# A transformer step on one core: u and v in program order, the matvec's finishing step moved, and ACT's weight conversions queued behind attention's copies

## Chip, core and metric

The kernel runs on one core of a Trainium2 chip. The metric is the device time of one execution in microseconds; before the change three runs took 1706.94, 1707.95 and 1711.22 us, median 1707.95. A separate execution was profiled; it took 1710.82 us.

## What is computed

One layer of a hybrid backbone for 128 context tokens and 256 latent tokens, 384 in all, model width 2048, in float32:

```python
mod = silu(cond) @ ada_w + ada_b            # 6 vectors of 2048 for each of two conditions
h   = rmsnorm(x, norm_w[0]) * (1 + scale_a) + shift_a
q, k, v, o, g, u = split(h @ w_in)          # 8 heads x 128, 32 gates, 1024 pooled channels
hm  = bidirectional_mlstm(q, k, v, g) ; hm = rmsnorm(hm) * sigmoid(o)
hp  = centred_pooling(u) @ pool_w * pool_scale
x   = x + gate_a * rmsnorm(concat(hm, hp) @ w_out, norm_w[1])
h   = rmsnorm(x, norm_w[2]) * (1 + scale_f) + shift_f
y   = square(relu(h @ w1)) @ w2             # hidden width 8192
x   = x + gate_f * rmsnorm(y, norm_w[3])
```

The outputs are x for all tokens and the final states of the mLSTM of the context tokens.

## The kernel before

Every large product is done in three fp32r products: the weights and the activations are each split into a rounded part `hi` and a rest `lo`, and `hi*hi`, `hi*lo` and `lo*hi` are added up in PSUM (`mm3`, L140). For the weights `load_w` (L120) does this for each tile of 128 x 1024: a DMA issued by SP into one of three `raw` buffers, a copy on ACT that rounds (L132), a subtraction on DVE (L133); there are four buffers (`N_W`) of `hi` and four of `lo`. So the conversion of a tile can begin when PE is through with the tile four before it.

**u and v (L391 to L423).** The work on w_in's columns u and v runs in 8 steps of 256 rows (two k of 128). Each step has five chunks of columns: u0, u512 (512 columns), v0, v3 (3 heads of 128) and v6 (2 heads and the 32 gates). A chunk is 18 matmuls: two k, three token tiles, three products. Its sums are added to SBUF by DVE (by ACT in step 0). Before a step can begin, its 256 rows of h must be there: `make_h` (L355) multiplies x by `mod` and adds the shift, on DVE (`hm`, L361; `hl`, L367) and ACT (`hh`, L366).

Those values of `mod` come from a matvec on PE with `ada_w`, a generator (`ada_mat`, L209) that is advanced by `next(ada0)`. Nine calls make one step's worth: eight load one piece of 512 KB each (four buffers) and multiply it on PE (8 small matmuls, L226); with the eighth comes the copy of the sums to `ada_sb` on ACT (L232); the ninth, here called the finishing step, does four more matmuls on `ada_sb` (L235) and adds up `mod` on DVE (L243, L248). `ADA_STEPS = (4, 0, 5, 0, 0)` says how many calls come behind each chunk: four behind u0, five behind v0. `make_h` of the next step is written behind the matmuls of v3 (`ci == 3`).

**Who orders the instructions.** The opening of the kernel, up to `order.close()` (L388), is inside a `manual_schedule` of PE, DVE and ACT: these engines do what is written there in the order in which it is written. Outside, a planner orders each engine's instructions ahead of time, from costs and due times, in the main by their place in the program. Every engine then executes its own list in order: an instruction that waits holds all that stands behind it in the list of its engine. `tc.issue_after(ins)` asks that what is written under it comes behind `ins` in the list of that engine.

The transposes of x (`transpose_x`, L327: three on PE per k, one copy on ACT or DVE) for the last seven k stand behind `order.close()`.

**q, k, o and what is fed between (L164, L696 to L742).** `gemm_T` goes through a product in tiles of 24 matmuls; after each tile it calls `feeds`, generators that add other work. While q and k of heads pair g are computed, the feeds do the gates and the pooling (g = 0), or the attention of the pair before (`attention`, L556): `decays` (matmul `mb`, L573; exponentials on ACT, L575), scores, state updates (`update`, L607; the sums of the context tokens are copied from PSUM by ACT to `C`, L615), outputs, and in the ninth call a transpose to `hT` with a copy by ACT to `hnT` (L686). The gates' generator (L463) transposes `aS`, `bS` and `gS` in its third call (`ps_col`, L527), which need exponentials that ACT does in its second.

Of the kernel before, what the change touches and what calls it, by code (L numbers as in the profile page):

```python
# [9 lines left out]
AF = mybir.ActivationFunctionType  # L10
# [5 lines left out]
KT = D // P  # L16
NTOK = 384
# [10 lines left out]
N_W = 4  # L28
N_ADA = 4
N_E = 1  # L30
ADA_STEPS = (4, 0, 5, 0, 0)
X_ORDER = "tatatatabtatatatat"
N_X = 4
RATE_GF = 0.4
RATE_GS = 0.25
S_FIRST, S_LAST, N_LAST = 1, 6, 2
RATES = (1.5, 1.3, 1.3)
RATE_MAT = 0.35

# [2 lines left out]
def hymba_kernel(  # L42
# [6 lines left out]
    nc = tc.nc  # L49
# [13 lines left out]
    def bank(name):  # L63
        return psum.tile([P, 512], F32, tag="ps", name=name)
# [50 lines left out]
    mw = prmT[:, 64:72]  # L115
# [4 lines left out]
    def load_w(pieces, name, n=1024, after=(), later=None):  # L120

        raw = wp.tile([P, 1024], F32, tag="raw", name=f"raw_{name}", bufs=3)
        a = pieces[0][1].shape[1]
        rv = raw[:, 0:n].rearrange("p (a b) -> p a b", a=a)
        for off, src in pieces:
            load_w.ins = nc.sync.dma_start(rv[:, :, off:off + src.shape[2]], src).ins
        hi = wp.tile([P, 1024], F32R, tag="hi", name=f"hi_{name}", bufs=N_W)
        lo = wp.tile([P, 1024], F32R, tag="lo", name=f"lo_{name}", bufs=N_W)
        with ExitStack() as es:
            for ins in after:  # L130
                es.enter_context(tc.issue_after(ins))
            nc.scalar.activation(hi[:, 0:n], raw[:, 0:n], AF.Copy)  # L132
            low = lambda: nc.vector.tensor_tensor(lo[:, 0:n], raw[:, 0:n], hi[:, 0:n].bitcast(F32), op=ALU.subtract)  # L133
            if later is None:
                low()
            else:
                later.append(low)
        return (hi[:, 0:n].rearrange("p (a b) -> p a b", a=a), lo[:, 0:n].rearrange("p (a b) -> p a b", a=a))
# [9 lines left out]
    class Feed:  # L148
# [11 lines left out]
        def finish(self):  # L160
            for _ in self.gen:
                pass

    def gemm_T(w, cols, xs, n, evac, feeds=(), korder=(0, 1, 2, 3), name="g", hold=None):  # L164

        wv = wview(w)
        acc = {}
        for g, c0 in enumerate(cols):
            for o in range(2):
                acc[g, o] = bank(f"acc_{name}_{c0}_{o}")  # L170
        for ki, kc in enumerate(korder):
            for g, c0 in enumerate(cols):
                hi, lo = load_w([(0, wv[:, 4 * kc:4 * kc + 4, c0:c0 + 256])], f"{name}_{c0}_{kc}", after=hold(ki, g) if hold else ())
                for k in range(4):
                    xh, xl = xs(4 * kc + k)
                    for o in range(2):
                        mm3(acc[g, o][:, 0:n], hi[:, k, o * P:(o + 1) * P], lo[:, k, o * P:(o + 1) * P],
                            xh[:, 0:n], xl[:, 0:n], ki == 0 and k == 0, ki == 3 and k == 3)
                for f in feeds:
                    f()  # L180
        for g, c0 in enumerate(cols):
            for o in range(2):
                evac(c0 // P + o, acc[g, o])
# [122 lines left out]
    ada0 = first_ada()  # L306
# [14 lines left out]
    xT = []  # L321
# [5 lines left out]
    def transpose_x(k):  # L327
        ps = bank(f"xt_{k}")
        for i in range(3):
            nc.tensor.transpose(ps[:, i * P:(i + 1) * P], x_tok[i][:, k * P:(k + 1) * P], ident)  # L330
        t = slot(f"xT{k}")
        if k % 2:
            nc.scalar.activation(t[:, 0:NTOK], ps[:, 0:NTOK], AF.Copy)
        else:
            nc.vector.tensor_copy(t[:, 0:NTOK], ps[:, 0:NTOK])
        xT.append(t)
# [34 lines left out]
    def load_chunk(s, ci, after=(), later=None):  # L371
        kind, c0, w = chunks[ci]
        ks = slice(ksteps[s][0], sum(ksteps[s]))
        if kind == "u":
            n, pieces = w, [(0, wv_in[:, ks, U0 + c0:U0 + c0 + w])]
        else:
            n, pieces = w * P, [(0, wv_in[:, ks, V0 + c0 * P:V0 + (c0 + w) * P])]
            if c0 == 6:
                pieces.append((n, wv_in[:, ks, 4 * M:4 * M + 32]))
                n += 32  # L380
        return load_w(pieces, f"{kind}_{c0}_{s}", ksteps[s][1] * n, after, later) + (n,)
# [4 lines left out]
    h_ins = make_h(0)  # L386
    lo_later[0]()
    order.close()  # L388
    for k in range(len(xT), KT):
        transpose_x(k)  # L390
    for s in range(NS):  # L391
        for ci, (kind, c0, w) in enumerate(chunks):
            k0, nk = ksteps[s]
            hi, lo, n = w_first if s == 0 and ci < 2 else load_chunk(s, ci, h_ins if s == 0 else ())
            if s == NS - 1 and ci == 4:
                with tc.issue_after(load_w.ins):
                    nc.sync.dma_start(masks, cs_src[:, 3:N_CST])
            acc = [bank(f"{kind}_{c0}_{s}_{i}") for i in range(3)]

            ways = ((0, 0), (1, 0), (0, 1))  # L400
            for ps in [ways[n:n + 1] for n in range(3)] if s == ci == 0 else [ways]:
                for k in range(nk):
                    for i in range(3):
                        for a, b in ps:
                            nc.tensor.matmul(acc[i][:, 0:n], h[k0 + k][a][:, i * P:(i + 1) * P], (hi, lo)[b][:, k, :],  # L405
                                             start=k == 0 and a + b == 0, stop=k == nk - 1 and b == 1)
            if s == ci == 0:
                w_first = load_chunk(0, 1, h_ins)
            for _ in range(ADA_STEPS[ci]):
                next(ada0, None)  # L410
            if ci == 3 and s < NS - 1:
                make_h(s + 1)
            for i in range(3):
                if kind == "u":
                    dst, src = u_sb[i][:, c0:c0 + w], acc[i][:, 0:n]
                else:
                    dst, src = vsb[i][:, c0:c0 + w, 0:128], acc[i][:, 0:w * P].rearrange("p (h e) -> p h e", e=P)
                if s == 0:
                    nc.scalar.activation(dst, src, AF.Copy)
                else:  # L420
                    nc.vector.tensor_tensor(dst, src, dst, op=ALU.add)
                if kind == "v" and c0 == 6:
                    nc.vector.tensor_tensor(gsb[:, i, :], acc[i][:, w * P:n], gbias if s == 0 else gsb[:, i, :], op=ALU.add)  # L423

    hx = lambda k: h[k]


    mix = [None] * KT
# [34 lines left out]
    def gates():  # L463
# [6 lines left out]
        for i in range(3):  # L470
            f = fg[:, i]
# [28 lines left out]
        for s in range(3):  # L500
            for d in range(2):
# [4 lines left out]
                if s < 2:  # L506
                    out = mnew[r] if s == 0 else mprev[r, tokc[d][2]:tokc[d][2] + 1]
# [12 lines left out]
        for d, cols in ((0, slice(0, 32)), (1, slice(32, 40))):  # L520
            nc.vector.tensor_scalar(gd[:, cols], ident[0:40, cols], gS[0:40, 1 + d, last[d]:last[d] + 1], None, op0=ALU.mult)
        yield
        for src, dst in ((aS, acol), (bS, ecol), (gS, gcol)):
            ps = bank("ps_col")
            i0 = 1 if dst is gcol else 0
            for i in range(i0, 3):
                nc.tensor.transpose(ps[:, i * 40:(i + 1) * 40], src[0:40, i, :], ident[0:40, 0:40])  # L527
            pv = ps[:, 0:120].rearrange("p (i r) -> p i r", r=40)
            for d in range(2):
                out = dst[:, :, :, d] if dst is ecol else dst[:, i0:, d, :]  # L530
                nc.vector.tensor_copy(out, pv[:, i0:, 32 * d:32 * d + 8])
        ps = bank("ps_n0")
# [23 lines left out]
    def attention(hp):  # L556
# [50 lines left out]
        def update(i, d, wk):  # L607

            out = att.tile([P, 2, 129], F32, tag="C", name=f"C1_{hp}_{i}_{d}", bufs=5)
            ps = bank(f"cu_{hp}_{i}_{d}")  # L610
            pv = ps[:, 0:258].rearrange("p (h e) -> p h e", e=129)
            for hl in range(2):
                nc.tensor.matmul(pv[:, hl, :], wk[:, hl, :], vsb[i][:, h0 + hl, :], start=True, stop=True)
            if i == 0:
                nc.scalar.activation(out, pv, AF.Copy)  # L615
            else:
                for hl in range(2):
                    nc.vector.scalar_tensor_tensor(out[:, hl, :], C0[d][:, hl, :], glast[:, 32 * d + h0 + hl:32 * d + h0 + hl + 1], pv[:, hl, :], op0=ALU.mult, op1=ALU.add)
            return out
# [60 lines left out]
        for hl in range(2):  # L680
            hd = h0 + hl
            ps = bank(f"hT_{hp}_{hl}")
            for i in range(3):
                nc.tensor.transpose(ps[:, i * P:(i + 1) * P], hss[i][:, hl, :], ident)
            mix[hd] = slot(f"hnT{hd}")
            nc.scalar.activation(mix[hd][:, 0:NTOK], ps[:, 0:NTOK], AF.Copy, scale=mw[:, hd:hd + 1])  # L686
        yield

    def mid_vec():
# [597 lines left out]
```

## Time and profile before

| | |
|---|---|
| median of three runs | 1707.95 us (1706.94 to 1711.22) |
| the profiled execution | 1710.82 us, span of its instructions 1709.0 us, mean granted clock 0.995 |
| PE busy | 1670.3 us, 98% |
| DVE, ACT, POOL busy | 1342.1 us (79%), 750.1 us (44%), 154.7 us (9%) |
| DMA | 320.95 MB, mean 188 GB/s |

The engines are PE (TensorE; PEld is its loading of weights, which overlaps), DVE (VectorE), ACT (ScalarE), POOL (GpSimd) and SP, which issues DMAs; a "q" behind an engine's name is its sequencer. Times in rows are microseconds from the first instruction, and L405 is line 405 of the kernel. A matmul's duration in a row is modelled and overlaps the next one; how fast matmuls follow one another is seen from their starts. The granted clock is 1.00 where TensorE has 2.4 GHz and 0.50 where it has 1.2.

### The profile page before, as it was taken

The page shows a single profiled execution, that of the slowest core. Times are in us where ns is not written, and L with a number is a line of the kernel's source. Part 1 is how long each engine was busy: PE and PEld are TensorE (multiplying, and loading weights), DVE is VectorE, ACT ScalarE, POOL GpSimd, SP SyncE. Part 2 cuts the span into 40 slices and gives each one's busy share as a digit, 9 for nine tenths or more (in the row PEclk, how much of TensorE's full clock was granted, in tenths as well). Part 3 has the DMA queues.
Part 4 walks back from the last instruction along what each step waited for, and adds up shares of the span by engine and source line. Part 5 has one row for each costly group of instructions (what it writes and reads, how often), then busy time and mean ns, then how long its engine had stood idle before and what let it go on. Part 6 is the DMA issues. An engine that isn't in the chain of part 4 may idle for free.

```text
span 1709.0 us, 28009 instructions
## 1 busy us (share of the span) xinstructions
PE 1670.3 (98%) x11021; PEld 1585.8 (93%) x11021; DVE 1342.1 (79%) x2000; ACT 750.1 (44%) x1224; POOL 154.7 (9%) x194
## 2 busy tenths in 40 slices
PE   6999999999999999999999999999999999999997
PEld 3777899898999999988999999999999999999996
DVE  3676749798889969999699588988488588588688
ACT  4332344555433336543444444444444444444443
POOL 0000001211101133440000000000000000000120
PEclk9999999999999999999999999999999999999999
DMA  9988857677688883664555344644443533533653
GB/s 300 309 278 284 283 154 252 212 236 226 226 281 292 264 280 111 182 194 130 154 185 168 116 148 129 198 136 126 134 135 105 156 120 113 162 107 117 186 185 135
DMA packets 262291, 320.95 MB, mean 188 GB/s; under 512 B 14752, under 2 KB 231440, under 8 KB 261776
## 3 DMA queue, kind: packets, MB, share of 16 engines
q1 hardware_dynamic: 254640, 303.61, 55.7%
q0 software_dynamic: 5856, 13.69, 2.8%
q8 instruction: 86, 1.41, 0.3%
q10 hardware_dynamic: 1664, 1.87, 0.3%
q14 instruction: 45, 0.37, 0.1%
HBM read 308.61 MB, written 10.51 MB: 187 GB/s over the span
## 4 chain that ended last, share of the span: by engine, by line
PE 79%; DVE 8%; DMA 6%; issue 4%; ACT 1%; POOL 1%; SPq 1%; DVEq 0%; ACTq 0%; POOLq 0%
PE acc_w L141 9%; PE acc_w L142 9%; PE acc_w L143 9%; PE y L1121 4%; PE y L1122 4%; PE y L1120 4%; PE v L405 3%; PE u L405 2%; PE y_yz L1120 2%; PE y_yz L1121 2%; PE y_yz L1122 2%; PE acc_wo L141 2%; PE acc_wo L143 2%; PE acc_wo L142 2%; DVE ada_acc L276 2%
## 5 line engine op out<-in xcount | busy, mean ns | idle before, releaser
L142 PE MATMUL acc_w<-h2l,hi_w 128*128 128x384 f32 (+1 forms) x1024 | 346.0, 338 | 0.5 <-DVE h2l L914 0.5
L143 PE MATMUL acc_w<-h2h,lo_w 128*128 128x384 f32 (+1 forms) x1024 | 345.8, 338 | 0.0
L141 PE MATMUL acc_w<-h2h,hi_w 128*128 128x384 f32 (+1 forms) x1024 | 344.6, 338 | 1.2 <-ACT h2h L910 1.2
L133 DVE TENSOR_TENSOR lo_w<-raw_w,hi_w 128x1024 fp32r<-128x1024 f32 x152 | 185.3, 1221 | 136.2 <-ACT hi_w L132 135.9
L276 DVE SCALAR_TENSOR_TENSOR ada_acc<-ada_raw,sg,ada_acc 128x1024 f32<-128x1024 f32 (+1 forms) x240 | 259.8, 1113 | 4.7 <-DMA ada_raw<-in_ada_w_dram 4.7
L132 ACT ACTIVATE hi_w<-raw_w 128x1024 fp32r<-128x1024 f32 x152 | 160.8, 1058 | 214.2 <-PE acc_w L142 93.9
L141 PEld LDWEIGHTS acc_w<-h2h,hi_w 128*128 128x128 f32 x1024 | 192.1, 188 | 2.9 <-ACT h2h L910 2.0
L142 PEld LDWEIGHTS acc_w<-h2l,hi_w 128*128 128x128 f32 x1024 | 192.6, 188 | 1.2 <-DVE h2l L914 0.8
L143 PEld LDWEIGHTS acc_w<-h2h,lo_w 128*128 128x128 f32 x1024 | 192.4, 188 | 0.3 <-DVE lo_w L133 0.2
L1106 ACT ACTIVATE hi_t<-w 128x1024 fp32r<-128x1024 f32 x104 | 109.5, 1060 | 117.7 <-DVE w L1142 33.0
L1107 DVE TENSOR_TENSOR lo_t<-w,hi_t 128x1024 fp32r<-128x1024 f32 x104 | 126.4, 1221 | 14.9 <-ACT hi_t L1106 14.6
L1107 DVE TENSOR_TENSOR lo_b<-w,hi_b 128x1024 fp32r<-128x1024 f32 x78 | 95.2, 1222 | 39.0 <-ACT hi_b L1106 38.7
L1106 ACT ACTIVATE hi_b<-w 128x1024 fp32r<-128x1024 f32 x78 | 82.5, 1060 | 96.7 <-PE acc_w L142 64.1
L132 ACT ACTIVATE hi_wo<-raw_wo 128x1024 fp32r<-128x1024 f32 x32 | 34.0, 1063 | 78.0 <-DMA raw_wo<-in_w_out_dram 43.2
L840 ACT ACTIVATE z<-acc_w 128x384 f32<-128x384 f32 x54 | 26.3, 487 | 75.1 <-PE acc_w L143 75.1
L876 POOL DMA_DIRECT2D gf_dram<-gfT x1 | 0.5, 521 | 551.6 <-DVE gfT L875 551.6
L405 PE MATMUL v<-hi_v,hh 128*128 128x384 f32 (+1 forms) x144 | 48.3, 335 | 0.2 <-ACT hi_v L132 0.2
L133 DVE TENSOR_TENSOR lo_wo<-raw_wo,hi_wo 128x1024 fp32r<-128x1024 f32 x32 | 40.3, 1267 | 9.1 <-ACT hi_wo L132 9.0
L405 PE MATMUL v<-hi_v,hl 128*128 128x384 f32 (+1 forms) x144 | 47.4, 329 | 0.0
L226 PE MATMUL ada<-ada_raw,cT 128*32 128x256 f32 x656 | 45.3, 393 | 1.8 <-DMA ada_raw<-in_ada_w_dram 1.8
L405 PE MATMUL v<-lo_v,hh 128*128 128x384 f32 (+1 forms) x144 | 47.0, 328 | 0.0
L141 PE MATMUL acc_k<-hh,hi_k 128*128 128x384 f32 x128 | 44.4, 347 | 0.7 <-ACT C L615 0.7
(2250 smaller groups left out, 4580.4 us busy)
## 6 DMA issues: line engine op xcount, KB each, us to landing
ada_raw<-in_ada_w_dram SPq DMA_DIRECT2D x170, 512.0 KB, 4.9
raw_w<-in_w_dram SPq DMA_DIRECT2D x152, 512.0 KB, 4.1
w<-in_w_dram SPq DMA_DIRECT2D x104, 512.0 KB, 4.1
raw_wo<-in_w_out_dram SPq DMA_DIRECT2D x32, 512.0 KB, 5.2
raw_u<-in_w_in_dram SPq DMA_DIRECT2D x16, 512.0 KB, 8.7
raw_q<-in_w_in_dram SPq DMA_DIRECT2D x16, 512.0 KB, 4.7
raw_k<-in_w_in_dram SPq DMA_DIRECT2D x16, 512.0 KB, 4.9
raw_o<-in_w_in_dram SPq DMA_DIRECT2D x16, 512.0 KB, 4.7
```

What stands on the lines that cost most here:

```text
L132: nc.scalar.activation(hi[:, 0:n], raw[:, 0:n], AF.Copy)
L133: low = lambda: nc.vector.tensor_tensor(lo[:, 0:n], raw[:, 0:n], hi[:, 0:n].bitcast(F32), op=ALU.subtract)
L141: nc.tensor.matmul(ps, lh, rh, start=start, stop=False)
L142: nc.tensor.matmul(ps, lh, rl, start=False, stop=False)
L143: mm3.ins = nc.tensor.matmul(ps, ll, rh, start=False, stop=stop).ins
L276: nc.vector.scalar_tensor_tensor(acc[:, g, :], raw[:, a, :], cj, acc[:, g, :], op0=ALU.mult, op1=ALU.add)
L405: nc.tensor.matmul(acc[i][:, 0:n], h[k0 + k][a][:, i * P:(i + 1) * P], (hi, lo)[b][:, k, :], start=k == 0 and a + b == 0, stop=k == nk - 1 ...
L1106: nc.scalar.activation(hi, raw, AF.Copy)
L1107: nc.vector.tensor_tensor(lo, raw, hi.bitcast(F32), op=ALU.subtract)
L1120: nc.tensor.matmul(acc, xh, wh, start=start and j == 0, stop=False)
L1121: nc.tensor.matmul(acc, xh, wl, start=False, stop=False)
L1122: nc.tensor.matmul(acc, xl, wh, start=False, stop=stop and j == 3)
```

## The change

There are four edits.

1. From the last of the opening's instructions to the end of the steps of u and v, PE alone is in a `manual_schedule`; the other engines stay with the planner. The seven transposes of x are now written behind the matmuls of u0 of step 0 (`XT_AT = 0`).
2. `ADA_STEPS` becomes `(4, 0, 4, 0, 0)`, and the ninth call, the finishing step, comes in the middle of the matmuls of v3, between its two k.
3. The gates' generator has one more `yield` ahead of the transposes to `ps_col`.
4. `gemm_T` keeps a list of what was done after each tile (`steps_done`). Attention's `C` copies and `hnT` copies put themselves on it, and the ACT conversion of a weight tile is queued behind those of four tiles ahead (`LAG = 4`).

```diff
+XT_AT = 0
-ADA_STEPS = (4, 0, 5, 0, 0)
+ADA_STEPS = (4, 0, 4, 0, 0)
+LAG = 4
...
+    steps_done = []
...
+        beside = hold or (lambda ki, g: steps_done[-LAG] if len(steps_done) >= LAG else ())
...
-                hi, lo = load_w([(0, wv[:, 4 * kc:4 * kc + 4, c0:c0 + 256])], f"{name}_{c0}_{kc}", after=hold(ki, g) if hold else ())
+                hi, lo = load_w([(0, wv[:, 4 * kc:4 * kc + 4, c0:c0 + 256])], f"{name}_{c0}_{kc}", after=beside(ki, g))
...
+                steps_done.append([])
                 for f in feeds:
...
     order.close()
-    for k in range(len(xT), KT):
-        transpose_x(k)
+    order2 = ExitStack()
+    order2.enter_context(tc.manual_schedule(engines={mybir.EngineType.PE}))
     for s in range(NS):
...
+                    if ci == 3 and k == 0:
+                        next(ada0, None)
             if s == ci == 0:
                 w_first = load_chunk(0, 1, h_ins)
+            if s == 0 and ci == XT_AT:
+                while len(xT) < KT:
+                    transpose_x(len(xT))
...
+    order2.close()
     hx = lambda k: h[k]
...
         yield
+        yield
         for src, dst in ((aS, acol), (bS, ecol), (gS, gcol)):
...
-                nc.scalar.activation(out, pv, AF.Copy)
+                steps_done[-1].append(nc.scalar.activation(out, pv, AF.Copy).ins)
...
-            nc.scalar.activation(mix[hd][:, 0:NTOK], ps[:, 0:NTOK], AF.Copy, scale=mw[:, hd:hd + 1])
+            steps_done[-1].append(nc.scalar.activation(mix[hd][:, 0:NTOK], ps[:, 0:NTOK], AF.Copy, scale=mw[:, hd:hd + 1]).ins)
```

## Rows read from the trace of the kernel before

**Rows 1.** Windows, steps 1 to 6: us, busy by engine, clock, DMA share, GB/s.

```profile
53.53:75.32 21.79, 21.79 (x160) 17.60 (x159) 14.73 (x33) 6.89 (x12) 0.00 (x0) 1.00 0.89 295
75.32:98.04 22.72, 22.64 (x160) 17.62 (x159) 16.66 (x34) 7.29 (x11) 0.00 (x0) 1.00 0.93 309
98.04:120.36 22.32, 21.88 (x160) 17.60 (x159) 16.33 (x36) 6.36 (x10) 0.42 (x1) 1.00 0.85 282
120.36:145.11 24.75, 23.43 (x160) 19.09 (x159) 17.63 (x39) 6.38 (x11) 0.84 (x2) 0.93 0.87 294
145.11:167.80 22.69, 21.89 (x161) 17.60 (x160) 14.78 (x31) 6.35 (x10) 0.00 (x0) 1.00 0.75 246
167.80:190.74 22.94, 21.88 (x161) 17.58 (x159) 15.93 (x34) 7.00 (x11) 0.00 (x0) 1.00 0.81 264
```

**Rows 2.** Waits of PE: waiter, releaser, us in total, times, longest.

```profile
PE ada L235 <- ACT ada_sb L232: 3.6, 4, 1.3
...
PE mb L573 <- ACT hnT L686: 1.6, 1, 1.6
...
PE ps_col L527 <- issue: 1.0, 1, 1.0
...
PE acc_k L141 <- ACT C L615: 0.7, 1, 0.7
```

**Rows 3.** Timeline of PE, steps 4 and 6: start, us, what, idle before.

```profile
135.90 0.44 PE L405 MATMUL v<-hi_v,hh 128*128 128x384 f32 x1
...
138.01 0.61 PE L235 MATMUL ada<-cst,ada_sb 128*128 128x4 f32 x4 [1.32 <-ACT ada_sb L232]
...
183.31 0.44 PE L405 MATMUL v<-hi_v,hh 128*128 128x384 f32 x1
...
185.16 0.61 PE L235 MATMUL ada<-cst,ada_sb 128*128 128x4 f32 x4 [1.06 <-ACT ada_sb L232]
```

**Rows 4.** Timelines of ACT, PE and DVE, end of step 3.

```profile
113.42 1.06 ACT L132 ACTIVATE hi_u<-raw_u 128x1024 fp32r<-128x1024 f32 x1 [9.85 <-DMA raw_u<-in_w_in_dram]
114.38 0.37 ACT L232 ACTIVATE ada_sb<-ada 128x256 f32<-128x256 f32 x1
...
114.80 0.61 PE L235 MATMUL ada<-cst,ada_sb 128*128 128x4 f32 x4 [0.44 <-ACT ada_sb L232]
...
117.63 0.34 PE L405 MATMUL v<-hi_v,hl 128*128 128x384 f32 x1
117.81 0.34 PE L405 MATMUL v<-lo_v,hh 128*128 128x384 f32 x1
...
120.36 0.40 PE L405 MATMUL u<-hi_u,hh 128*128 128x512 f32 x1
...
115.99 1.23 DVE L133 TENSOR_TENSOR lo_u<-raw_u,hi_u 128x1024 fp32r<-128x1024 f32 x1
...
118.45 1.40 DVE L367 SCALAR_TENSOR_TENSOR hl<-hm,mod,hh 128x128 fp32r<-128x128 f32 x4
```

**Rows 5.** Timeline of PE, step 0.

```profile
28.77 2.38 PE L330 MATMUL xt<-cst,xtok 128*128 128x128 f32 x20
...
33.40 0.72 PE L405 MATMUL u<-lo_u,hh 128*128 128x512 f32 x2
...
35.91 1.93 PE L226 MATMUL ada<-ada_raw,cT 128*32 128x256 f32 x32
```

**Rows 6.** Windows, three stretches of low clock: columns as in rows 1.

```profile
139.82:143.23 3.41, 3.41 (x13) 3.41 (x12) 3.41 (x10) 1.60 (x4) 0.53 (x2) 0.50 1.08 365
228.56:231.97 3.41, 3.41 (x20) 2.60 (x20) 1.66 (x5) 1.44 (x3) 0.00 (x0) 0.50 0.51 143
317.31:320.72 3.41, 3.41 (x12) 3.41 (x11) 3.41 (x6) 2.67 (x11) 0.12 (x1) 0.50 0.87 262
```

**Rows 7.** Timeline of ACT, second pair of heads.

```profile
314.88 1.06 ACT L132 ACTIVATE hi_k<-raw_k 128x1024 fp32r<-128x1024 f32 x1 [2.98 <-PE acc_q L142]
...
315.84 1.04 ACT L686 ACTIVATE hnT<-hT,prmT 128x384 f32<-128x384 f32 x2
```

## The prediction

> **What bounds the kernel now.** I read the page first: its first part has TensorE busy for 98% of the span, so a microsecond is to be had only where TensorE stands still or runs at half clock. The list of waits of PE then names the places that the change touches: four waits of the matvec's finishing step for its copy on ACT, one of `mb` for ACT's `hnT`, one of `ps_col`, and one of `acc_k` for ACT's `C` [rows 2]. Third, the table of windows, cut at the first u matmul of each of the steps of u and v, gives what such a step costs as a whole [rows 1]: step 1 takes 21.79 us with PE busy throughout, steps 2 to 6 take 22.72, 22.32, 24.75, 22.69 and 22.94. Fourth, the timeline shows the order of the instructions around each of these waits [rows 3, 4, 5, 7], and a second table of windows the stretches with the granted clock at 0.50, that is at 1.2 instead of 2.4 GHz [rows 6]. Each of three of them follows shortly on one of these waits: 139.82 on the finishing step that waited until 138.01 [rows 3], 228.56 on the 1.0 us of `ps_col`, 317.31 on the 1.6 us of `mb` [rows 2]. Work of 3.41 us at half clock is 1.7 us of work, so each fall costs 1.7 us beside the wait.
>
> **The change part by part.**
>
> *The finishing step of the matvec.* Now it stands behind three matmuls of the chunk v3 and waits for `ada_sb`, which ACT starts only when `hi_u` of the next step, itself waiting for its load, is through: 113.42 to 114.38 [rows 4]. The change puts it behind nine matmuls of v3, six later. They start 0.18 us apart (117.63 to 117.81) [rows 4], so in step 4 it comes at 135.90 + 9 x 0.18 = 137.52 and `ada_sb` lets it go at 138.01: 0.49 us of the wait stay. In step 6 it comes at 183.31 + 1.62 = 184.93 against 185.16: 0.23 us stay [rows 3]. In step 3 it comes at 115.2 against 114.80: nothing stays. I take step 1 as the length of a step without such waits; steps 2 to 6 are longer by 0.93 + 0.53 + 2.96 + 0.90 + 1.15 = 6.47 us [rows 1], in which the first fall of the clock is contained (step 4, clock 0.93). Less the 0.72 that stay, the gain is 5.75 us. A part of step 2's 0.93 is that the planner cut one matvec group in two; program order keeps it whole, provided that its loads are there.
>
> What is late next: `hm`, `hh`, `hl` of the next step hang on the finishing step. In step 3 they take from 114.80 to the second pair of `hl`, of which the first pair is done halfway through the four that begin at 118.45 and last 1.40: 119.15, or 4.35 us behind the finishing step, with a `lo_u` of 1.23 in between. The next u matmul is at 120.36, 5.56 behind it [rows 4]. With six v matmuls fewer between them 5.56 - 6 x 0.18 = 4.5 us are left, and the second u matmul, the first that reads `hl`, is another matmul later. That is cover of 0.2 to 0.4 us. DVE's order is the planner's still: a second subtraction of 1.23 ahead of `hm` would use it up and cost about 1.0 in that step. Bounds: nothing, or seven steps x 1.0 = 7.0 us. I take 1.0 in all, one step of seven, since the cover is positive in the step whose rows I read.
>
> *PE in program order.* Before, the planner's order was nearly that of the program. What really moves are the seven transposes of x of step 0: 20 of their matmuls ran from 28.77 for 2.38 us, while PE waited for the first h anyway [rows 5]. Afterwards they come behind the first u chunk. That chunk ends sooner: from 33.40, when `lo_u` let PE go on, ten of its matmuls ran until 35.91, 0.25 us each, and in program order only the six of its last pass are left by then, so it ends 4 x 0.25 = 1.0 us sooner. The matvec group that started at 35.91 [rows 5] starts 2.38 - 1.0, about 1.3 us, later. It frees the four buffers of the loads, so loads and the rest of step 0 follow. Bounds: 1.0 gained (the earlier end of u, if the transposes fall into waits behind it) and 2.4 lost. I take 1.3 lost. SP's queue issues the same loads in the planner's order; PSUM holds three banks of u, those of x and one of the matvec, and what frees them are seven short copies on ACT and DVE, which I count at nothing: if PE waited for one of them, it would be for half a microsecond, inside the bounds.
>
> *Gates: one more `yield`.* The transposes of `bS` and `gS` come one tile later. The 1.0 us of `ps_col` [rows 2] goes, since a tile of q or k is 24 matmuls, 4.3 us at 0.18, and with it, I expect, the fall at 228.56: 1.0 + 1.7 = 2.7 us. At worst the small matmuls make the same fall one tile later: then 1.0. Who needs them, `decays` of the first heads, comes a whole q and k later.
>
> *Attention: hi conversions behind the copies.* At 314.88 ACT takes `hi_k`, which had waited in its queue for a buffer, and only then, at 315.84, the two `hnT` copies whose PSUM banks PE needs [rows 7]. The change queues that conversion (the tile four ahead) behind them: the 1.6 of `mb` and the 0.7 of `acc_k` for `C` [rows 2] go, and the fall at 317.31 with them: 1.6 + 0.7 + 1.7 = 4.0 us. Behind the copies the conversion waits about 1.0 us (two copies, 1.04 [rows 7]); its tile is used three tiles later, which hides it. If a copy is itself late, ACT's whole queue stands behind the conversion; there are eight such tiles, and 1.0 us each, if nothing hides it, is 8.0. I take nothing; the range of this part is from 8.0 lost to 4.0 gained.
>
> *Sum.* 5.75 + 2.7 + 4.0 - 1.0 - 1.3 = 10.15 us, against the profiled execution's own 1710.82 (span 1709.0 and 1.8 around it): 1700.7. The median of the runs is 1707.95, 2.9 below that execution. I take the difference for falls of the clock that those runs had fewer of (1.7 each); then 5.1 - 2.9 = 2.2 of the 5.1 us of falls is left to be gained, the sum against the median is 7.2, and the time again about 1700.7. I predict **1700.5**.
>
> **A rule to weigh.** The windows show the 16 DMA engines busy for 0.75 to 0.93 of steps 1 to 6, at 246 to 309 GB/s, and PE's weight loads for 17.60 of 21.79 us, 0.81, in step 1 [rows 1]. The Trainium skill (Perfetto Trace Analysis, Identifying the Most-Contended Engine) says not to trust matmul busy time, to judge TensorE by its weight loads, and to work on the most contended engine first. By that rule the steps of u and v belong to the loads as much as to TensorE, and taking away waits of PE would return nothing there; the sum by it is that of the first rival.
>
> **The rivals.**
> - *The loads bound the steps.* Mechanism here: the matvec's four buffers and the three of u and v are refilled when PE and DVE free them, so a PE that waits less finds the next load less early, and the wait moves from the finishing step to a load. For it: 0.93 DMA share in step 2. Against it: step 1 did 21.79 us at 295 GB/s without a wait, and step 2 shows 309 [rows 1]. At 309 the 295 x 21.79 = 6430 KB of a step take 20.8 us, a microsecond less than PE needs. Then the 5.75 is not gained: 10.15 - 5.75 = 4.4, 1706.4 by the profiled execution; with the falls that the median lacks, 1705.5.
> - *The clock falls elsewhere.* The waits go, but three falls come behind others of the small waits that stay. For it: falls follow waits of 1.0 to 1.6 us, and a new order may make one of that length anywhere. Against it: the 0.7 of `acc_k` [rows 2] has no fall behind it now. 10.15 - 5.1 = 5.0: 1705.7 by the profiled execution, and by the median 7.2 - 2.2 gives 1703.
> - *The chain to h decides, and the kernel is slower.* Place: the first u matmuls of steps 1 to 7, where PE, in a fixed order, has nothing to put in front. Price: 1.0 to 1.2 us in each of seven steps (a subtraction of 1.23 ahead of `hm`), 8.4, and as such waits are as long as those that fall the clock now, four falls, 6.8. It decides as soon as the cover is below zero in most steps. The gain of 7.2 against the median counts 1.0 for this chain; with 8.4 in its place and 6.8 of falls the time is 1707.95 - 7.2 + 7.4 + 6.8 = 1715.
> - *The change does not do what it says*: conversions of ACT other than those behind which it queues hold the copies, or `ada_sb` stays late by as much as the step moves. Then only gates remain, 1.0 to 2.7: 1706.
>
> **How the numbers follow.** My forecast's case 0.58 (its own range 1697 to 1704), loads 0.14, clock elsewhere 0.12, chain to h 0.08, not as it says 0.08. A new order of one engine changes what the planner does with the others: waits of PE in the attention and output stretch that no part touches may come or go by 3 us, which is in the ranges. About 5.1 us, 0.3%, is what a measurement can tell from no change: faster means below 1702.8, slower above 1713.1. Faster: 0.58 x 0.9 plus about a third of loads, clock and the last = 0.62. Slower: 0.07, from the chain to h. The same: 0.31. The range from 1695 (no loss in step 0 or on the chain to h, and 3 us of luck: 1700.5 - 2.3 - 3) to 1707.5 (loads, and 2 us against) leaves out the chain to h and the ends of the others.
>
> **What would show it.** Right: the waits of PE no longer list `ada L235` by more than 1 us, nor `mb` for `hnT`; the steps from 1 on last 21.8 to 22.3 each; step 0 ends about 1 us later; no clock at 0.50 near 139, 228 and 317. Wrong: u waiting for `hl` or `lo_u` at each step's beginning, or `ada L226` for its loads; a low clock after other waits; `lo_q`, `lo_k` late in the attention tiles.

## The result, and the profile after

The changed kernel takes **1697.56 us**, median of six runs (1693.3 to 1699.63); six runs of the kernel before beside them have a median of 1707.9 (1706.94 to 1713.73). The ratio is 0.9933, with a 95% interval of 0.9918 to 0.9947: faster by 0.7%. That is 2.9 us below the forecast of 1700.5 and inside its range. The profiled execution took 1699.63 us, span 1697.8, against 1710.82 and 1709.0; the mean granted clock is 0.998 where it was 0.995.

The windows of the changed kernel, cut like [rows 1] and with the same columns: step 0, steps 1 to 6, a low-clock stretch, and then the stretch of q and k with attention (first matmul of k to the first of o) and the one ahead of it (last of u and v to the first of k).

```profile
30.26:56.13 25.87, 25.86 (x179) 21.26 (x180) 13.00 (x26) 16.16 (x31) 0.00 (x0) 0.93 0.89 290
56.13:78.50 22.37, 22.02 (x161) 17.46 (x160) 13.97 (x30) 6.95 (x13) 0.00 (x0) 1.00 0.90 293
78.50:100.15 21.65, 21.65 (x161) 17.65 (x159) 16.19 (x35) 6.51 (x11) 0.00 (x0) 1.00 0.86 284
100.15:121.75 21.60, 21.60 (x161) 17.64 (x159) 16.13 (x35) 6.30 (x11) 0.00 (x0) 1.00 0.88 287
121.75:144.07 22.32, 22.05 (x161) 17.52 (x159) 15.10 (x32) 5.24 (x9) 0.42 (x1) 1.00 0.91 294
144.07:166.61 22.54, 22.15 (x159) 17.70 (x159) 16.79 (x38) 7.33 (x13) 0.84 (x2) 1.00 0.85 280
166.61:188.91 22.30, 21.92 (x161) 17.48 (x160) 15.95 (x35) 7.19 (x12) 0.00 (x0) 1.00 0.81 263
31.10:34.51 3.41, 3.41 (x9) 2.63 (x8) 3.32 (x5) 1.26 (x2) 0.00 (x0) 0.50 1.05 339
...
233.95:397.80 163.85, 163.07 (x1063) 155.28 (x1063) 138.50 (x231) 82.83 (x218) 30.76 (x27) 1.00 0.74 232
205.78:233.95 28.17, 28.17 (x203) 26.60 (x201) 17.89 (x48) 13.97 (x23) 1.84 (x3) 1.00 0.65 206
```

Steps 1 to 6 take 132.78 us together where [rows 1] add up to 137.21: 4.43 less. Two of them, 21.65 and 21.60, have no wait at all. Step 0 takes 25.87; before it took 22.62. The three falls of [rows 6] are gone, and there is a new one at 31.10. Step 0 and the same two last windows of the kernel before:

```profile
30.91:53.53 22.62, 22.30 (x161) 17.55 (x160) 11.69 (x25) 14.44 (x30) 0.00 (x0) 1.00 0.92 300
...
238.56:408.55 169.99, 165.55 (x1064) 157.05 (x1063) 138.85 (x232) 82.67 (x221) 30.96 (x27) 0.99 0.70 224
207.62:238.56 30.94, 29.94 (x202) 27.85 (x201) 17.52 (x48) 14.19 (x23) 1.84 (x3) 0.94 0.59 184
```

So attention's stretch became 6.14 us shorter and the gates' 2.77. The account of the two profiled spans: first u 0.65 sooner, step 0 longer by 3.25, steps 1 to 6 shorter by 4.43, step 7 the same, gates shorter by 2.77, attention 6.14, all that follows (1300.45 us before, 1300.0 after) 0.45; in sum 11.2, which is the difference of the spans.

The waits of PE in the changed kernel, columns as in [rows 2]:

```profile
...
PE acc_wo L145 <- DVE lo_wo L135: 1.9, 2, 1.1
PE ada L232 <- DMA ada_raw<-in_ada_w_dram: 1.5, 2, 1.1
PE u L411 <- ACT hh L372: 1.4, 1, 1.4
PE acc_w L143 <- ACT h2h L923: 1.2, 2, 0.7
PE ada L241 <- ACT ada_sb L238: 0.9, 3, 0.4
...
PE u L411 <- DVE hl L373: 0.4, 1, 0.4
...
```

`mb` for `hnT`, `acc_k` for `C` and `ps_col` are no longer listed; the finishing step waits 0.9 us in three places instead of 3.6. New are the 1.4 us for `hh` and the 0.4 for `hl`. The 1.9 of `acc_wo` (0.8 before) came after the stretches above; another execution of the changed kernel (a2 below) shows 1.0 there. In attention, the timeline of ACT shows the edit at work, against [rows 7]: the two `hnT` copies start as soon as PE has delivered, and the conversion comes behind them.

```profile
308.54 1.05 ACT L699 ACTIVATE hnT<-hT,prmT 128x384 f32<-128x384 f32 x2 [1.75 <-PE hT L697]
309.48 3.21 ACT L588 ACTIVATE e<-mb,acol 128x128 f32<-128x128 f32 x12
312.49 1.16 ACT L134 ACTIVATE hi_k<-raw_k 128x1024 fp32r<-128x1024 f32 x1
```

### The profile page after: what moved, and what is told of

Same layout as the page of the kernel before. It is cut to its first block, busy times and chain, and to the rows that moved or that the text cites. A ratio compares the mean times of both kernels' runs of the same rounds, so it can differ in the third digit from the quotient of the medians.

```text
span 1697.8 us, 28001 instructions
## 1 busy us (share of the span) xinstructions
PE 1664.2 (98%) x11021; PEld 1581.1 (93%) x11021; DVE 1341.8 (79%) x2000; ACT 750.9 (44%) x1224; POOL 155.9 (9%) x194
## 3 DMA queue, kind: packets, MB, share of 16 engines
q8 instruction: 86, 1.41, 0.3%
## 4 chain that ended last, share of the span: by engine, by line
PE 68%; DVE 15%; DMA 8%; issue 6%; ACT 1%; POOL 1%; SPq 0%; DVEq 0%; ACTq 0%; POOLq 0%
PE acc_w L145 9%; PE acc_w L143 9%; PE acc_w L144 9%; DVE ada_acc L282 6%; PE y L1134 4%; PE y L1135 4%; PE y L1133 4%; PE u L411 2%; DMA raw_u<-in_w_in_dram 2%; PE v L411 2%; PE y_yz L1133 2%; PE y_yz L1134 2%; PE y_yz L1135 2%; PE y L975 2%; PE y L977 2%
## 5 line engine op out<-in xcount | busy, mean ns | idle before, releaser
L134 ACT ACTIVATE hi_u<-raw_u 128x1024 fp32r<-128x1024 f32 x16 | 16.8, 1058 | 63.7 <-DMA raw_u<-in_w_in_dram 62.5
```

## The experiments

The question was which edit pays what, whether the parts add up, and what the late transposes cost. My theory: three places pay separately, and the loss in step 0 is that of the transposes' new place. Rivals: the gain is mostly that of clock falls, which any of the edits may take away; and PE's program order pays or costs by itself. Each line of the table is the median of the runs, with the ratio to runs of the kernel before on the same chip.

| kernel | us | ratio, 95% |
|---|---|---|
| e1: edits 1 and 2 alone | 1704.45 | 0.9987 (0.9978 to 0.9996) |
| e2: edit 3 alone | 1704.41 | 0.9985 (0.9972 to 0.9999) |
| e3: edit 4 alone | 1701.37 | 0.9964 (0.9951 to 0.9976) |
| e4: all, transposes ahead of u0 | 1694.89 | 0.9929 (0.9916 to 0.9943) |
| e9: all, four transposes ahead, three behind | 1696.94 | 0.9936 (0.9922 to 0.9949) |
| e5: all, finishing step in its old place | 1703.34 | 0.9978 (0.9968 to 0.9988) |
| e7: all, finishing step behind v3 | 1701.73 | 0.9972 (0.9962 to 0.9982) |
| e6: all, without program order | 1695.89 | 0.9934 (0.9921 to 0.9948) |
| e11: e6 again | 1695.22 | 0.9921 (0.9905 to 0.9937) |
| a2: the changed kernel again | 1698.82 | 0.9936 (0.9918 to 0.9953) |
| e10: edits 3 and 4 | 1699.89 | 0.9948 (0.9931 to 0.9966) |
| e8: the kernel before again, one run | 1709.2 | |

**One part alone.** e1 is the kernel before with

```diff
-ADA_STEPS = (4, 0, 5, 0, 0)
+XT_AT = 0
+ADA_STEPS = (4, 0, 4, 0, 0)
...
+    order2.enter_context(tc.manual_schedule(engines={mybir.EngineType.PE}))
...
+                    if ci == 3 and k == 0:
+                        next(ada0, None)
```

> The kernel before with edits 1 and 2 alone (PE in program order over u and v, finishing step in the middle of v3); gates and attention as before. Theory, that the three places pay separately: the first u matmul to the last v matmul's place in the span moves as in the changed kernel, 207.6 to 205.8, so 1.8 us less in a profile whose kernel before had a fall of the clock there; waits of mb for hnT and of ps_col stay, with their falls; about 1706.0. Rival, that the gain is a single one (a new order upstream shifts everything): 1700 or less, and the waits of mb and ps_col are gone or short here too.

e2 has only the gates' `yield`:

```diff
         yield
+        yield
```

> The kernel before with edit 3 alone (one more yield in the gates' generator). Theory: the 1.0 us wait of ps_col and the fall at 228.56 go, 2.7 us, about 1705.2; the waits of ada L235 and of mb stay. Rival, that the wait only moves with ps_col to the next tile, or the fall comes anyway: 1707 to 1708, and a low clock within 10 us behind the new place of ps_col.

e3 has only the order of ACT (`LAG`, `steps_done`, `beside`; the main line of it):

```diff
-... after=hold(ki, g) if hold else ())
+... after=beside(ki, g))
```

> The kernel before with edit 4 alone (conversions queued behind the C and hnT copies of four tiles ahead). Theory: the waits of mb for hnT (1.6) and of acc_k for C (0.7) go, the fall at 317 with them; in the changed kernel the stretch from 303.7 to 408.6 shrank by 6.0 us, so 4.0 to 6.0 less: 1702 to 1704. Rival, that another wait of the same length takes the place (hT for hs, inter for hs): 1706 to 1708.

Against 1707.42 they gain 3.0, 3.0 and 6.0 us by the medians, in sum 12.0 (2.2, 2.6 and 6.1 by the ratios); all together gained 10.3. Within their intervals the parts add up. Each came out somewhat faster than I had expected, by 1.6 us (e1), 0.8 (e2) and 0.6 beyond the range (e3). In e1 and e3 the waits of the places that the edit doesn't touch stay. In e1:

```profile
PE mb L580 <- ACT hnT L693: 1.5, 3, 0.8
PE u L406 <- ACT hh L367: 1.4, 1, 1.4
...
PE ps_col L534 <- issue: 1.0, 1, 1.0
...
PE acc_k L142 <- ACT C L622: 0.9, 1, 0.9
```

And in e3, where `mb` and `acc_k` are gone:

```profile
PE ada L240 <- ACT ada_sb L237: 2.7, 5, 1.0
...
PE ps_col L532 <- issue: 1.0, 1, 1.0
```

e2's profile is less clean: `ps_col` is gone, but the finishing step's 3.6 us are 2.5 there and the 1.6 of `mb` are 0.5, which the edit doesn't touch, and its execution, 1700.84 us, was the fastest of its twelve. So one profile of e2 can't be read as the price of edit 3. The profiles of e2 and e3 show no low clock at all before the end of the kernel, e3's with the 1.0 us of `ps_col` in it. That spoke against the price that I had given to the waits, and asked for e8.

**The kernel before once more (e8).** Nothing is changed in it.

> The kernel before, profiled a second time. Theory one, each fall of the clock belongs to a wait of PE: falls again near 139.8, 228.6 and 317.3, span 1709. Theory two, the same waits do not always fall the clock: other places or fewer falls, and the span shorter by 1.7 for each that is missing (1704 with none).

Its two finishing steps with a wait above 1.2 us, from the timeline of PE:

```profile
115.97 0.61 PE L235 MATMUL ada<-cst,ada_sb 128*128 128x4 f32 x4 [1.38 <-ACT ada_sb L232]
...
140.96 0.61 PE L235 MATMUL ada<-cst,ada_sb 128*128 128x4 f32 x4 [1.40 <-ACT ada_sb L232]
```

And its windows of the attention and of the gates stretch:

```profile
239.59:406.63 167.04, 163.87 (x1064) 155.52 (x1063) 138.87 (x232) 82.79 (x221) 30.96 (x27) 1.00 0.73 228
210.26:239.59 29.33, 28.32 (x202) 26.66 (x201) 17.78 (x48) 14.19 (x23) 1.84 (x3) 1.00 0.63 198
```

The clock fell to 0.50 at 117.60 and at 141.49, behind these two waits, and nowhere else before the end of the kernel; `ps_col` waited its 1.0 us and `mb` 1.1 us with the clock at 1.00. So the place decides less than I had assumed: of the falls of [rows 6], the one behind the finishing step comes back, in two steps now, the other two don't. Without its fall the gates stretch is 29.33 instead of 30.94, 1.6 us for the fall with the wait the same, and attention's 167.04 instead of 169.99.

**The transposes (e4, e9).** e4 is the changed kernel with all seven ahead of the first u chunk, e9 with four of them there and three behind it:

```diff
     order2.enter_context(tc.manual_schedule(engines={mybir.EngineType.PE}))
+    while len(xT) < KT:         # e9: for _ in range(4)
+        transpose_x(len(xT))
...
-            if s == 0 and ci == XT_AT:     # e4 drops these three lines, e9 the first
-                while len(xT) < KT:
-                    transpose_x(len(xT))
```

> The changed kernel, but with the seven transposes of x in PE's program order ahead of u0 of step 0 instead of behind it. Theory, that step 0 lost 2.6 us because the transposes had filled a wait (they now cost their own 2.4 behind u0, and the wait of 1.4 for hh that they filled brought a fall at 31.1): u0 begins near 31.0, the low clock at 31 is gone, step 1 begins near 53.5 instead of 56.1, the kernel 2 to 3.5 us faster than the changed one: about 1694.8. Rival, that step 0 is set by its loads and the transposes' place does not matter: step 1 begins near 56 again, 1697.5.

> The changed kernel with four of the seven transposes of x in PE's order ahead of u0 of step 0 and three behind it. With all seven ahead, u0 waited 1.8 us for PSUM banks that ACT's copies of xT held. Theory: four fill the 1.4 us until hh is there, banks are free, three behind u0 cost 1.0: step 1 begins near 53.5 to 54, 1 us sooner than with all seven ahead, about 1693.9. Rival, that banks or the loads set step 0 whatever the order: step 1 begins at 54.9 or later, 1695 or more.

The timeline of PE in step 0, first of the changed kernel, then of e4:

```profile
28.24 0.61 PE L241 MATMUL ada<-cst,ada_sb 128*128 128x4 f32 x4
30.26 2.75 PE L411 MATMUL u<-hi_u,hh 128*128 128x512 f32 x6 [1.41 <-ACT hh L372]
32.81 2.33 PE L411 MATMUL u<-hi_u,hl 128*128 128x512 f32 x6
34.98 1.55 PE L411 MATMUL u<-lo_u,hh 128*128 128x512 f32 x6
36.37 2.45 PE L336 MATMUL xt<-cst,xtok 128*128 128x128 f32 x21
```

```profile
28.99 2.38 PE L335 MATMUL xt<-cst,xtok 128*128 128x128 f32 x20
31.12 0.48 PE L412 MATMUL u<-hi_u,hh 128*128 128x512 f32 x1
32.11 0.50 PE L412 MATMUL u<-hi_u,hh 128*128 128x512 f32 x1 [0.50 <-ACT xT L338]
33.43 1.20 PE L412 MATMUL u<-hi_u,hh 128*128 128x512 f32 x4 [0.82 <-ACT xT L338]
34.47 1.55 PE L412 MATMUL u<-hi_u,hl 128*128 128x512 f32 x6
```

In the changed kernel PE stands still for 1.41 us in front of the first u, and then its first two passes of six matmuls take 2.55 and 2.17 us, 0.43 and 0.36 from start to start, where e4's last two rows go at 0.26 and 0.23: that is the low clock. e4 fills the wait with the transposes, and pays 0.50 and 0.82 for their copies, which hold the PSUM banks that u needs. Its step 1 starts at 54.94, e9's at 53.53, that of the changed kernel at 56.13. By the medians e4 is 2.7 us ahead and e9 0.6; by the ratios e4 is ahead by 0.7 and e9 not at all. The intervals overlap, so the runs give the sign for e4 with little certainty and settle nothing for e9. e9's step 1 began where I had expected it, and its time, 1696.94, is still 3 us above the 1693.9; in its profile u waited 1.45 us for `lo_u` in step 7, at 192.16, and that step took 2.0 us more than in the changed kernel.

e5 and e7 below have the same order in step 0 as the changed kernel and the same wait of 1.41 us, but no fall of the clock behind it. Their step 1 starts at 55.49 and 54.97, where it starts at 56.13 with the fall.

**The finishing step's place (e5, e7).** e5 puts it back to where v3 begins, e7 puts it behind all 18 matmuls of v3:

```diff
-ADA_STEPS = (4, 0, 4, 0, 0)
+ADA_STEPS = (4, 0, 5, 0, 0)     # e5; e7: (4, 0, 4, 1, 0)
...
-                    if ci == 3 and k == 0:
-                        next(ada0, None)
```

> The changed kernel with the finishing step back where it was written before, behind the matvec group after v0 and ahead of v3 (five calls behind v0); PE still in program order. Theory, that the place of the finishing step is what pays in the steps of u and v: PE now stands from the group's end to the end of ACT's ada_sb with nothing between, as long as from the start of v3 to the finishing step in the kernel before, 0.8 to 2.1 us in each of seven steps, about 9 in all against 1.3 now, and falls of the clock behind the longer ones: 1705 to 1711. Rival, that program order alone pays and the finishing step is hidden either way: 1697 to 1699, and waits of the finishing step below 2 us in total.

> The changed kernel with the finishing step later still, behind all 18 matmuls of v3. Theory, that the chain from the finishing step over mod, hm, hh to hl is 4.35 us long and only just covered: nine v matmuls, 1.6 us, fewer cover it, so each of seven steps begins 1.0 to 1.5 us late with u waiting for hh or hl, 7 to 10 us in all and falls of the clock beside: 1704 to 1712; the waits for ada_sb vanish. Rival, that the planner shortens the chain when it is the last to end, by setting the subtraction for u behind it: 1698 to 1701.

Both lose against the changed kernel: 5.8 us in e5, 4.2 in e7. That is less than I had expected: both medians lie below the ranges of the theory (1705 and 1704 at their lower ends), and above those of the rivals. In e5 the finishing step waits 6.6 us in seven places (I had said about 9); the two longest, from the timeline of PE:

```profile
73.08 0.61 PE L241 MATMUL ada<-cst,ada_sb 128*128 128x4 f32 x4 [1.96 <-ACT ada_sb L238]
...
120.94 0.61 PE L241 MATMUL ada<-cst,ada_sb 128*128 128x4 f32 x4 [2.15 <-ACT ada_sb L238]
```

Here the clock fell behind both (74.06 and 121.84). In e7 the finishing step doesn't wait, but the next step's first matmuls do, in five of seven steps and without a fall; from the timeline of PE at the start of step 5:

```profile
147.04 0.50 PE L411 MATMUL u<-hi_u,hh 128*128 128x512 f32 x1 [0.95 <-ACT hh L372]
147.93 0.50 PE L411 MATMUL u<-hi_u,hl 128*128 128x512 f32 x1 [0.39 <-DVE hl L373]
```

From the finishing step to the next u are 6.1 us in e5, 4.4 in the changed kernel and 2.8 in e7, without waits. 2.8 is too little for the chain to h in five of seven steps; 4.4 is just enough in all but one.

**Program order, and the missing cell (e6, e11, e10).** e6 and e11 are the changed kernel with PE left to the planner and the transposes where they were; e10 has the steps of u and v as before, and edits 3 and 4.

```diff
-    order2 = ExitStack()
-    order2.enter_context(tc.manual_schedule(engines={mybir.EngineType.PE}))
+    for k in range(len(xT), KT):
+        transpose_x(k)
...
-            if s == 0 and ci == XT_AT:
-                while len(xT) < KT:
-                    transpose_x(len(xT))
...
-    order2.close()
```

> The changed kernel without PE's program order: the finishing step is written in the middle of v3, gates and attention as changed, but the planner orders PE over u and v and the transposes of x stand ahead of the steps as before. Theory, that the later place of the finishing step is enough and program order cost step 0 its filled wait: step 1 begins near 53.5, the finishing step's waits are at most 1.3 us in total, 1694 to 1696. Rival, that the planner moves the finishing step ahead again behind three matmuls of v3, so that the waits of 3.6 stay: 1698 to 1700, still with step 1 near 53.5.

> The changed kernel without the program order of PE, again, for a narrower interval: 1695.9 as in its first run if the planner's order is the better one by 1.5 us; 1697 to 1697.5 if the two are the same. In the profile: steps 1 to 7 of 21.6 each, no finishing step that waits.

> The changed kernel again, beside the two others on one chip. If program order costs nothing beside the planner's order: within 0.7 us of the run below. If it costs what the two profiles show (first u of step 1 at 56.13 against 53.6): 1.5 to 3 us more, about 1697.5. Its profile should show the wait of 1.4 us for hh at the start of step 0 again, since order is fixed; if a fall of the clock follows a given wait each time, it falls near 31 again; if falls differ among executions, it need not.

> Only the edits of the gates and of the attention (3 and 4), the steps of u and v as before: the missing cell beside old place in program order (1703.34), new place in the planner's order (1695.89) and both new (1697.56). If the parts add up, 1707.5 - 3.0 (gates alone) - 6.0 (attention alone) = 1698.5: then program order with the old place costs about 5 us of its own (1703.3 - 1698.5), and the new place is worth 2.6 in the planner's order and 5.8 in program order. Rival: the place is worth 6 us in any order, and this kernel takes about 1702 to 1703; the gains of gates and attention alone then overlap. The profile should show the finishing step waiting for its copy by 2.5 to 3.6 us in all, as before, and no waits of mb or of the gates' transposes.

| finishing step | planner's order | program order, late transposes |
|---|---|---|
| old place | 1699.89 (e10) | 1703.34 (e5) |
| new place | 1695.89, 1695.22 (e6, e11) | 1697.56, 1698.82 (changed kernel, a2) |

e10, e11 and a2 ran on one chip. The place is worth 4.0 to 4.7 us in the planner's order and 4.5 to 5.8 in program order: what I had expected of e10 (2.6 in the planner's order) is too little, and its rival (1702 to 1703) too slow. Program order with the transposes late costs 3.5 us in the old place and 1.7 to 3.6 in the new. In the old place part of that is the finishing step itself: the planner had put it three matmuls of v3 later than the program has it, 33 instead of 36 v matmuls ahead of the next u. In the new place the planner leaves it where it is written. Windows of e6, step 0 and step 1:

```profile
30.96:53.58 22.62, 22.41 (x162) 17.50 (x161) 11.43 (x24) 14.42 (x30) 0.00 (x0) 1.00 0.92 302
53.58:75.24 21.66, 21.66 (x160) 17.67 (x159) 14.11 (x30) 6.53 (x12) 0.00 (x0) 1.00 0.88 292
```

Step 0 is as short as before, and in this execution steps 1 to 6 take 21.6 to 21.8 each. In e11, the same kernel, steps 4 to 6 took 22.0 to 22.7, not the 21.6 that I had expected. a2 has the wait of 1.41 us for `hh` again, and the low clock behind it, at 30.45. The ten runs of e6 and e11 (1693.5 to 1696.9) lie below most of the twelve of the changed kernel (1693.3 to 1700.1; their median 1698.56); so the new place without program order is probably the better version, by some 3 us. On the one chip where both ran the intervals of the ratios overlap.

**All the profiles side by side.** The kept profiles, cut at the same places, separate by edit, whichever else was in the kernel. Lengths are in us.

| stretch | without the edit | with it |
|---|---|---|
| steps 1 to 6, finishing step in its new place | 134.4 to 140.1 (before, e8, e2, e3, e10, e5) | 129.9 to 132.8 (changed kernel, a2, e1, e4, e6, e9, e11) |
| gates stretch, edit 3 | 29.3 (e3, e8); 30.9 with a fall of the clock (before, e1) | 28.2 in nine, 29.1 in e6 |
| attention's stretch, edit 4 | 165.9 to 170.0 (before, e8, e1, e2) | 162.6 to 164.6 in ten |

In attention's stretch all waits of PE together are 2.2 to 4.4 us without edit 4 and 0 to 1.4 with it. In steps 1 to 6 the old place had falls in four of its six profiles, the new place in none of its seven; the two of the old place without a fall, e2 and e3, took 134.4 and 134.5. With the finishing step later still (e7) they took 138.3.

## Why the prediction was right

**The finishing step later (-5.75).** The mechanism was right. The profiles give 4.43 us over steps 1 to 6, with the chain's loss, of 0.88 below, in it: 5.3 by themselves; the pairs of runs give 4.0 to 5.8. A fall of the clock, 1.7, is in the 4.43: against e2 and e3, which have the old place and no fall, the changed kernel's steps are only 1.7 us shorter, those of a2 2.8 and those of e1 3.8. What I had let stay was 0.49 us in step 4 and 0.23 in step 6; the changed kernel lost 0.36 and 0.54 there, and 0.50 in step 1, from start to start. The base, step 1's length without waits, was nearly right: 21.79, and the two steps without waits took 21.60 and 21.65.

**The chain to h (+1.0).** Right in place and in size, but by luck: the cause was another. These are timelines of the changed kernel, of DVE at the end of step 3, where nothing was lost, then of ACT, DVE and PE at the end of step 4:

```profile
118.11 1.22 DVE L135 TENSOR_TENSOR lo_u<-raw_u,hi_u 128x1024 fp32r<-128x1024 f32 x1
...
137.95 1.06 ACT L134 ACTIVATE hi_u<-raw_u 128x1024 fp32r<-128x1024 f32 x1 [9.59 <-DMA raw_u<-in_w_in_dram]
138.91 0.37 ACT L238 ACTIVATE ada_sb<-ada 128x256 f32<-128x256 f32 x1
140.46 1.06 ACT L134 ACTIVATE hi_u<-raw_u 128x1024 fp32r<-128x1024 f32 x1 [1.18 <-DVE mod L249]
...
141.55 1.23 DVE L135 TENSOR_TENSOR lo_u<-raw_u,hi_u 128x1024 fp32r<-128x1024 f32 x1 [1.15 <-ACT hi_u L134]
142.69 0.15 DVE L254 SCALAR_TENSOR_TENSOR mod<-mod,prmT 128x4 f32<-128x4 f32 x1
...
143.24 1.40 DVE L367 SCALAR_TENSOR_TENSOR hm<-xT,mod,rbc 128x128 f32<-128x128 f32 x4
...
144.95 0.50 PE L411 MATMUL u<-hi_u,hl 128*128 128x512 f32 x1 [0.39 <-DVE hl L373]
```

I had feared a second subtraction ahead of `hm`. There is none: one `lo_u` stands between the first part of `mod` and `hm` in step 3 too, at 118.11, and costs nothing. In step 4 that `lo_u`, at 141.55, had to wait 1.15 us for ACT's `hi_u` of 140.46, and all that stands behind it in DVE's list waited with it. The row puts ACT's own wait down to `mod` on DVE, which `hi_u` doesn't read; in the trace its load landed at 140.38, 2.5 us behind that of the `hi_u` before it, where the two loads of step 3 landed 1.3 apart. So a late load held the chain. u came 0.23 late at 144.07 for `hh`, and the second u matmul 0.65 late for `hl`: 0.88 us, in this step alone.

**PE in program order (+1.3).** Right in sign, too small by half, and outside my bounds (2.4 lost): step 1 began 2.6 us later. The chunk u0 was to end a microsecond sooner; it ended at 36.37 instead of at 35.91, because the wait that the transposes had filled, 1.41 us, stands there now and the clock fell behind it. 18 matmuls at 0.23 from start to start would have been through at 34.4. I had priced the transposes' time and not the hole that they leave, nor the fall. Without the fall, in e5 and e7, step 1 began 2.0 and 1.4 us later than before; these two have the finishing step elsewhere, so the fall's share is not measured exactly. e4 and e6 show that with the transposes in the hole neither comes.

**Gates (-2.7).** The profiles give 2.77, but a fall of the clock is in it that came in only two of the four profiles with that wait: the stretch is 1.16 us shorter than in e8 and e3, which have no fall there. e2's median, 3.0 us, has an interval from 0.2 to 4.8 and can't tell the two apart.

**Attention (-4.0).** The waits went as I had said, and the part is larger than I had it: 6.14 us by the profiles, 6.0 by e3's median (4.1 to 8.4). One fall, which I counted, is in the 6.14. Against e8, without one, it is 3.2 us: there `mb` waited 1.1 instead of 1.6. What I had not counted are PE's waits in this stretch for `hs` and `C` of DVE, 2.1 us before and 0.8 after; they are smaller in nearly all profiles with edit 4, and why is open. Conversions that queue behind the copies hold nobody: `lo_q` and `lo_k` are not among the waits of PE in the changed kernel.

**The sum and the median.** -10.15 against the profiled execution's own time; the profiled execution after took 11.2 less. That they are so close is in part luck: the loss of step 0 was too small by 1.3, the gain of attention by 2.1. For the median I had cut the gain to 7.2, since its runs should have had fewer falls to lose; they gained 10.3. This correction is the term of the sum that was mis-sized by most, 3.1 us, and is what makes the forecast too high by 2.9. The profiled execution after lies above its median as well, by 2.1 us, so the distance from the profile to the median was not one of falls that only the kernel before has.

**The rivals.** Loads don't bound the steps: steps 2 and 3 took 21.65 and 21.60 us at 284 and 287 GB/s. They set the rest, though: `hi_u` at 137.95 had waited for its load, and `ada_sb` stood behind it on ACT. The Trainium skill (Perfetto Trace Analysis, Identifying the Most-Contended Engine) says to optimize the most contended engine first. That taking away waits of PE would return nothing, where the loads rank as high as TensorE, was my own reading and is not said there; these steps returned 4.43 us with the DMA share at 0.81 to 0.91. The clock fell in one new place, at 31.10, for the three that were lost. The chain to h decided nothing here, and does in e7. Of the signs that I had named, the waits and the lost falls came; the steps spread wider than 21.8 to 22.3 (21.60 to 22.54), and step 0 ended 2.6 us later and not 1.

## What to carry to other kernels

Where an in-order engine has a step that waits for another engine, move it back until the chain that hangs on it runs out of cover, and no further: here 6.1 us ahead of the consumer waited for its input, 4.4 fitted, and 2.8 made the consumer wait. Before an engine's order is fixed by hand, list what its scheduler had put into the waits; that work belongs into them still, and a wait laid bare can cost a fall of the clock on top. Queue bulk work, such as weight conversions, behind the small copies that free another engine's buffers when it has time to spare.

## What the runs showed of the hardware

- The same wait does not always bring the clock down. Behind finishing steps that waited 1.32 to 2.15 us (one in the kernel before, two in e8, two in e5, one in e10) it was at 0.50 for 3.41 us each time. Behind the 1.41 us for `hh` in step 0 it fell in e1, in the changed kernel and in a2, not in e5 and e7. Behind the 1.0 us of `ps_col` it fell in the kernel before and in e1, not in e8 and e3. Behind the 1.45 us of u for `lo_u` in e9 it did not fall. So in these profiles the length of the wait alone doesn't decide; a fall is a loss with a chance, and one profile doesn't show the chance.
- Two executions of one program differ by microseconds without a fall: the steps of u and v, first u to last v, took 169.75 us in e6 and 172.97 in e11, the same kernel on two chips. Of the difference 1.0 came in step 0, 0.7 in step 4 from a load that landed late, and most of the rest from waits for `hl` and `hh`. One profile can't price a change of 2 us in these steps.
